# Opening phase of a two-layer trunk: query, gates and half of the keys in seven open PSUM banks, adaLN sums two blocks ahead, gates on 128 partitions

## The chip, the cores and the metric

The kernel runs on one core of one Trainium2 chip. Everything is float32 in HBM. The metric is the device time of one execution in microseconds (us), from a median over several runs. TensorE (PE) multiplies matrices, VectorE (DVE), ScalarE (ACT) and GpSimd (POOL) work on tiles, and SyncE (SP) issues the loads.

## The reference, cut to what matters

A trunk of two layers on 512 tokens of width 1024. Layer 0 mixes the tokens with an mLSTM, layer 1 with a gated MLP; each is followed by a channel MLP. The change touches only the beginning of layer 0:

```python
c_act = silu(c)
mod = c_act @ ada_w[0] + ada_b[0]                # six vectors of 1024
sh1, sc1, g1, sh2, sc2, g2 = split(mod, 6)
h = rmsnorm(x, norm_g[0, 0]) * (1.0 + sc1) + sh1
p = h @ w_in                                     # (512, 3088)
q, k, v, o, ig, fg = split(p, [512, 1024, 2048, 3072, 3080])
ig = 15 * tanh((ig + b_i) / 15); fg = 15 * tanh((fg + b_f) / 15)
logf = log_sigmoid(fg)                           # 8 heads x 512 tokens
bcum = cumsum(logf)                              # inside each chunk of 128 tokens
# running maximum of ig - bcum in a chunk, then the stabilised weights of the mLSTM
```

## The kernel before, in words

Each product of float32 matrices is made of three products of rounded parts (`mm3`, line 248): both operands are split in a high part `hi` and a rest `lo`, and `hi*hi`, `hi*lo`, `lo*hi` are summed in one PSUM bank. ScalarE casts the high part of a weight tile, VectorE or GpSimd subtracts to get the low part (`conv`, line 221). PSUM has eight banks of 128x512: five of `bank()`, two of `bank2()`, one of `bank3()` (lines 76 to 82). Buffers for loaded blocks of 1 MB (`raw`) are five, buffers for adaLN sums (`R`) two, for converted weights (`whi`, `wlo`) four each.

Everything up to line 647 is pinned: each engine's queue follows the program's order exactly (class `Engine`, line 40 on). Behind `pinned[0] = False` a scheduler orders the instructions of each engine.

The input's 1024 columns are handled as eight blocks k of 128. For each block the columns of scale and shift are sums over 1024 rows of `ada_w`. `ada_load` (line 145) loads 1 MB in two DMAs. `ada_init` and `ada_acc` (lines 152 and 157) multiply eight slices by `cact` and add them in two accumulators: two ScalarE operations and six of VectorE on 128x256. `ada_merge` adds the two on GpSimd, `ada_tr` transposes the two halves on TensorE, and `ada_fin` (line 174) reduces each over its row and makes the two columns in four VectorE operations.

The function `mlstm` (line 531) opens with the load of adaLN block 0, the four tiles of x, the gate weights as four loads of narrow columns into zeroed tiles, and the first 128x512 blocks of the query weights. The tiles of x are normalized (sum of squares on ScalarE, power on GpSimd, scaling on VectorE). In the loop over k (line 623) each engine gets: sums of block k+2, columns of block k+1, load of k+3, scale and shift of block k+1 (`feed`, line 604: ScalarE affine, ScalarE cast, low part on GpSimd), query weights of k+1 (`q_hi` on ScalarE, `q_lo` on GpSimd), the 15 matmuls of block k (gates and four query tiles in five banks), and the two transposes of the sums and four of x (`xT`, line 590) for block k+2. The key projection follows the loop: four column tiles of 24 matmuls each, each in a bank of its own (lines 646 and 677).

The gates leave the loop as rows: 8 heads on partitions, 512 tokens along the row. The log sigmoid is a chain of some 16 operations on 8x512, then four transposes and copies turn it, four products with a triangle of ones make the cumulative sum, and the running maximum is seven steps of doubling distance, each a VectorE maximum and a ScalarE copy (lines 696 to 710). The results go to HBM and come back as broadcasts for the decays (`decay`, line 748). The values' projection (`proj_tm`) runs at the same time, the output gates (`o_unit`, line 801) after it.

## Time and profile before

| | us |
|---|---|
| median of 3 runs | 1270.68 |
| range of the runs | 1267.6 to 1271.62 |
| the profiled execution | 1269.99 |
| its span (first to last instruction) | 1268.2 |

| engine | busy us of the span | share |
|---|---|---|
| PE (matmul) | 1210.4 | 95% |
| PEld (weight load) | 986.0 | 78% |
| DVE | 848.0 | 67% |
| ACT | 619.5 | 49% |
| POOL | 129.2 | 10% |

All durations come from one profiled execution; its own time is the basis of sums, and the median lies 0.69 us above it. A matmul's end is modelled, so two matmuls that overlap in the rows are spaced by their starts. The shares are averages over stages with different limits, so a stage is read by itself. Nearly all instructions carry line 50, the helper that issues them, and are told apart by the names of their tiles: `raw` a loaded block, `r` an adaLN sum, `hhi` and `hlo` the two parts of the activations, `whi` and `wlo` those of weights, `pa` the bank of the sums, `pt` the banks of transposes, `ps` the banks of products.

### The profile page before, as it was taken

To read this page: it belongs to the slowest core of one execution; us is meant where nothing else is said; L and a number is where in the kernel's file an instruction comes from. 1 tells how busy PE (TensorE), PEld (TensorE's weight loads), DVE (VectorE), ACT (ScalarE), POOL (GpSimd) and SP (SyncE) were. 2 spreads that over 40 slices of the span, in tenths; PEclk is the share of its full clock that TensorE was granted. 3 is DMA by queue.
4 is the path that set the end of the run, shared out by engine and by line. 5 is a ranking of instruction groups with operands and counts; after the bars stand their busy time and mean duration, and the time that the engine had idled before them with its cause. 6 is when DMAs were issued, how large, how long until landed. Compare 5 with 4: busy or idle time off the path is not lost.

```text
span 1268.2 us, 15234 instructions
## 1 busy us (share of the span) xinstructions
PE 1210.4 (95%) x5705; PEld 986.0 (78%) x5705; DVE 848.0 (67%) x1360; ACT 619.5 (49%) x1107; POOL 129.2 (10%) x158
## 2 busy tenths in 40 slices
PE   2999998999999999999899999999999999999997
PEld 1678777888787887778678788888798888887886
DVE  5897677573967869866666756532747758668545
ACT  4545535285555545553653644322664554545432
POOL 4601211010000000010110023300100000000000
PEclk9999999999999999999999999999999999999999
DMA  9957942433354363365256644332443332331401
GB/s 262 307 185 193 264 127 89 141 125 103 105 166 133 101 198 111 93 213 176 97 154 212 206 119 137 128 108 67 133 133 108 109 125 66 122 111 51 148 1 67
DMA packets 165722, 174.24 MB, mean 137 GB/s; under 512 B 6152, under 2 KB 121080, under 8 KB 165648
## 3 DMA queue, kind: packets, MB, share of 16 engines
q1 hardware_dynamic: 165408, 173.17, 44.0%
q8 instruction: 45, 0.74, 0.2%
q14 instruction: 29, 0.24, 0.1%
q10 hardware_dynamic: 240, 0.09, 0.0%
HBM read 171.11 MB, written 2.14 MB: 137 GB/s over the span
## 4 chain that ended last, share of the span: by engine, by line
PE 70%; DVE 11%; DMA 7%; ACT 5%; issue 2%; POOL 2%; SPq 2%; DVEq 0%; POOLq 0%; ACTq 0%
PE ps L50 49%; PE pt L50 21%; DMA raw<-in_ada_w 5%; DVE wlo L50 3%; DVE a L50 3%; DVE r L50 2%; SPq L50 2%; ACT whi L50 2%; ACT j L50 2%; POOL s L50 1%; ACT t L50 1%; DMA a<-in_b_ws 1%; DVE x L50 1%; DMA raw<-in_a_w_in 1%; DVE s L50 1%
## 5 line engine op out<-in xcount | busy, mean ns | idle before, releaser
L50 DVE TENSOR_TENSOR wlo<-raw,whi 128x1024 fp32r<-128x1024 f32 x232 | 284.8, 1232 | 203.0 <-ACT whi L50 197.5
L50 PE MATMUL ps<-whi,a 128*128 128x512 f32 x1312 | 418.9, 394 | 0.5 <-DVE a L50 0.3
L50 ACT CAST whi<-raw 128x1024 fp32r<-128x1024 f32 x232 | 242.4, 1051 | 309.6 <-PE ps L50 220.4
L50 PEld LDWEIGHTS ps<-whi,a 128*128 128x128 f32 x1312 | 246.4, 188 | 61.8 <-DVE a L50 5.4
L50 PE MATMUL ps<-wlo,a 128*128 128x512 f32 x656 | 256.7, 392 | 0.0
L50 DVE SCALAR_TENSOR_TENSOR r<-raw,cact,r 128x256 f32<-128x256 f32 (+1 forms) x256 | 143.7, 599 | 26.1 <-ACT r L50 13.3
L50 PE MATMUL pt<-hhi,whi 128*128 128x512 f32 x384 | 150.7, 392 | 2.2 <-ACT t L50 1.3
L50 PE MATMUL pt<-hhi,wlo 128*128 128x512 f32 x384 | 149.9, 391 | 1.5 <-DVE wlo L50 1.5
L50 PE MATMUL pt<-hlo,whi 128*128 128x512 f32 x384 | 149.5, 389 | 0.0
L50 PEld LDWEIGHTS ps<-wlo,a 128*128 128x128 f32 x656 | 123.6, 188 | 25.3 <-DVE wlo L50 1.2
L50 PE MATMUL ps<-hlo,whi 128*128 128x512 f32 (+1 forms) x360 | 127.7, 355 | 2.4 <-POOL hlo L50 2.4
L50 PE MATMUL ps<-hhi,whi 128*128 128x512 f32 (+1 forms) x360 | 129.1, 359 | 0.3 <-ACT whi L50 0.3
L50 PE MATMUL ps<-hhi,wlo 128*128 128x512 f32 (+1 forms) x360 | 127.5, 354 | 0.7 <-DVE wlo L50 0.7
L50 DVE TENSOR_TENSOR a<-a,a 128x512 fp32r<-128x512 f32 (+2 forms) x162 | 105.1, 685 | 32.0 <-ACT a L50 31.7
L50 PE MATMUL ps<-wlo,hhi 128*128 128x512 f32 x256 | 102.6, 401 | 6.0 <-DVE wlo L50 5.8
L50 PE MATMUL ps<-whi,hhi 128*128 128x512 f32 x256 | 102.7, 402 | 2.1 <-ACT whi L50 2.1
L50 PE MATMUL ps<-whi,hlo 128*128 128x512 f32 x256 | 101.5, 396 | 0.0
L50 ACT CAST a<-a 128x512 fp32r<-128x512 f32 x108 | 63.2, 616 | 53.9 <-POOL a L50 41.8
L50 POOL TENSOR_TENSOR s<-s,mhalf 128x1 f32<-128x1 f32 (+1 forms) x40 | 32.4, 811 | 548.9 <-DVE s L50 541.6
L50 PEld LDWEIGHTS pt<-hhi,whi 128*128 128x128 f32 x384 | 72.1, 188 | 19.0 <-ACT whi L50 2.5
L50 PEld LDWEIGHTS pt<-hhi,wlo 128*128 128x128 f32 x384 | 72.1, 188 | 18.6 <-DVE wlo L50 3.7
L50 PEld LDWEIGHTS pt<-hlo,whi 128*128 128x128 f32 x384 | 72.1, 188 | 14.7
(128 smaller groups left out, 1376.8 us busy)
## 6 DMA issues: line engine op xcount, KB each, us to landing
raw<-in_ffn_w SPq DMA_DIRECT2D x64, 1024.0 KB, 5.1
raw<-in_ada_w SPq DMA_DIRECT2D x64, 512.0 KB, 5.5
raw<-in_ada_w SPq DMA_DIRECT2D x16, 1024.0 KB, 5.1
raw<-in_b_w_in SPq DMA_DIRECT2D x16, 1024.0 KB
raw<-in_a_w_in SPq DMA_DIRECT2D x10, 1024.0 KB, 10.2
raw<-in_b_w_out SPq DMA_DIRECT2D x8, 1024.0 KB, 5.0
raw<-in_a_w_out SPq DMA_DIRECT2D x4, 1024.0 KB, 5.0
x<-in_x SPq DMA_DIRECT2D x4, 512.0 KB, 6.5
```

The costliest lines, as they stand in the source:

```text
L50: r = f(*a, **k)
```

## The change

x is loaded first. Its tiles are normalized, transposed and copied into two `raw` buffers before the loop. The loads of a block are the adaLN block and 768 columns of weights (512 of the query, 256 of the keys), these in two DMAs. The adaLN sum has one accumulator: one ScalarE operation and seven on VectorE; two matmuls with a column of ones take the place of transposes, merge and reduction; scale and norm weight are joined in one operation. The loop has 21 matmuls for each block in seven banks (four query tiles, two key tiles, gates), all low parts are made on VectorE, and the sums of block k+2 are finished and those of k+3 begun in iteration k. Behind the loop two key blocks are left. The gates are turned first, so that the log sigmoid works on 128 tokens x 32; the running maximum is one scan. The adaLN columns of later sublayers go through `ada_fin` and the new `ada_cols`.

```diff
     def ada_fin(ps, l, vs, vc, ng, k):
         s = small(2)
         dve.tensor_reduce(s, ps[:, 0:2 * P].rearrange("p (a b) -> p a b", a=2), axis=AX.X, op=ALU.add)
-        ab = cp.tile([P, 4], F32, tag="ab", name=nm("ab"), bufs=16)
-        dve.tensor_scalar(ab[:, 2:3], s[:, 1:2], abcol(l, vc, k), 1.0, ALU.add, ALU.add)
+        return ada_cols(s, l, vs, vc, ng, k)
+
+    def ada_cols(s, l, vs, vc, ng, k):
+
+        ab = cp.tile([P, 2], F32, tag="ab", name=nm("ab"), bufs=16)
+        dve.tensor_scalar(ab[:, 1:2], s[:, 1:2], abcol(l, vc, k), ngcol(l, ng, k), ALU.add, ALU.mult)
         dve.tensor_add(ab[:, 0:1], s[:, 0:1], abcol(l, vs, k))
-        dve.tensor_mul(ab[:, 1:2], ab[:, 2:3], ngcol(l, ng, k))
...
+        def load(k):
+
+            raws[k] = ada_load(0, 0, 1, k)
+            raw = A(), A()[:, 0:QK - S]
+            ld.dma_start(raw[0], w[k * P:(k + 1) * P, 0:S])
+            ld.dma_start(raw[1], w[k * P:(k + 1) * P, S:QK])
+            qk[k] = [raw]
+
+        def qk_hi(k):
+            hi = wp.tile([P, QK], F32R, tag="whi", name=nm("whi"))
+            act.copy(hi[:, 0:S], qk[k][0][0])
+            act.copy(hi[:, S:QK], qk[k][0][1])
...
+        def init(k):
+            accs_[k] = R()[:, 0:2 * P]
+            act.activation(accs_[k], flat(k, KC - 1), AF.Copy, scale=cact[:, KC - 1:KC])
+
+        def sums(k, js=range(KC - 1)):
+            a = accs_[k]
+            for j in js:
+                dve.scalar_tensor_tensor(out=a, in0=flat(k, j), scalar=cact[:, j:j + 1], in1=a,
+                                         op0=ALU.mult, op1=ALU.add)
+
+        def total(k):
+
+            ps = bank3()
+            for i in range(2):
+                pe.matmul(ps[:, i:i + 1], lhsT=accs_[k][:, i * P:(i + 1) * P], rhs=one, start=True, stop=True)
+            return ps
...
+        x_stat(0)
+        x_stat(1)
+        x_turn(0)
+        x_stat(2)
+        x_turn(1)
+        x_out(0)
+        x_stat(3)
+        x_turn(2)
+        x_out(1)
         pt = bank2()
         for i in range(2):
             pe.transpose(out=pt[:, i * P:(i + 1) * P], in_=pk[:, i, :], identity=ident)
...
+        x_turn(3)
+        init(0)
+        x_out(2)
+        sums(0)
+        dve.tensor_copy(cols, pt[:, 0:2 * P].rearrange("p (a b) -> p a b", a=2))
+        scales = cols[:, 1, 0:96].rearrange("p (a b) -> p a b", b=KC)[:, 1::3, :]
+        dve.tensor_scalar_add(scales, scales, 1.0)
+        x_out(3)
+        sp0 = total(0)
...
+        qk_hi(0)
+        init(1)
+        qk_lo(0)
+        ab = [ada_cols(sp0, 0, 0, 1, 0, 0)]
+        full = feed_hi(0)
+        sums(1, range(3))
+        feed_lo(0, full)
+        sums(1, range(3, KC - 1))
+        wgc += [conv(wg[i]) for i in range(2)]
+        qk_hi(1)
+        init(2)
+        sums(2, range(2))
         for k in range(KC):
+            main(k, range(2))
+            if k + 1 < KC:
+                sp1 = total(k + 1)
+            main(k, range(2, 7))
+            if k + 3 < KC:
+                load(k + 3)
+            if k + 3 < KC:
+                init(k + 3)
+            if k + 1 < KC:
+                ab.append(ada_cols(sp1, 0, 0, 1, 0, k + 1))
+                qk_lo(k + 1)
+                full = feed_hi(k + 1)
             if k + 2 < KC:
-                ada_acc(raws[k + 2], accs_[k + 2], range(6))
+                sums(k + 2, range(2, 4))
             if k + 1 < KC:
-                ab.append(ada_fin(aps, 0, 0, 1, 0, k + 1))
+                feed_lo(k + 1, full)
+            if k + 2 < KC:
+                qk_hi(k + 2)
+                sums(k + 2, range(4, KC - 1))
             if k + 3 < KC:
...
+                sums(k + 3, range(2))
         pinned[0] = False
...
+        ps = bank2()
+        for n in range(NT):
+            pe.transpose(out=ps[:, n * 40:(n + 1) * 40], in_=gt[0:40, n * P:(n + 1) * P], identity=ident[0:40, 0:40])
+        scr = A()
+        fg, e, z, z2 = (scr[:, i * 32:(i + 1) * 32] for i in range(4))
...
+        kps = accs[4:6]
+        for blk in w_cols(w, QK):
+            kps.append(bank())
+            proj_fm(kps[-1], blk, h, slice(0, S))
...
-            pe.matmul(ps[0:8, n * P:(n + 1) * P], lhsT=lft[n], rhs=triu, start=True, stop=True)
+            pe.matmul(ps[0:8, n * P:(n + 1) * P], lhsT=logf[:, n * 8:(n + 1) * 8], rhs=triu, start=True, stop=True)
...
+        cm = A()[0:8]
+        dve.tensor_tensor_scan(cm, low, u, 0.0, ALU.add, ALU.max)
```

## Rows read from the trace of the kernel before

**Rows 1.** Busy time by stage: stretch, length, each engine's busy us (instructions), clock, DMA.
```profile
0.00:28.00 28.00, 4.39 (x15) 2.78 (x16) 15.65 (x33) 11.61 (x21) 12.76 (x29) 1.00 0.91 256
20.00:28.00 8.00, 1.64 (x7) 1.35 (x8) 7.27 (x13) 3.11 (x6) 3.02 (x4) 1.00 1.18 306
28.00:67.20 39.20, 36.31 (x159) 27.25 (x158) 32.74 (x64) 22.46 (x38) 24.05 (x21) 1.00 0.94 277
88.95:135.00 46.05, 45.83 (x209) 36.85 (x208) 33.87 (x70) 25.19 (x68) 8.24 (x24) 1.00 0.76 215
```

**Rows 2.** Timeline of TensorE, loop and keys: start, duration, engine, operation.
```profile
28.03 0.78 PE L50 MATMUL ps<-hhi,whi 128*128 128x512 f32 x1
...
33.47 0.38 PE L50 MATMUL pa<-ident,r 128*128 128x128 f32 x2
33.69 0.60 PE L50 MATMUL pt<-ident,a 128*128 128x128 f32 x4
...
34.05 0.48 PE L50 MATMUL ps<-hhi,whi 128*128 128x512 f32 x1
...
67.18 0.39 PE L50 MATMUL ps<-hhi,whi 128*128 128x512 f32 x1
...
88.94 0.39 PE L50 MATMUL ps<-whi,hhi 128*128 128x512 f32 x1
```

**Rows 3.** TensorE's waits, 28 to 67 us: us in total, times, longest.
```profile
PE ps L50 <- POOL hlo L50: 2.4, 3, 1.1
```

**Rows 4.** Timeline of VectorE's adaLN sums and GpSimd's subtractions beside them.
```profile
9.89 2.46 DVE L50 SCALAR_TENSOR_TENSOR r<-raw,cact,r 128x256 f32<-128x256 f32 x6 [5.77 <-DMA a<-in_a_hnorm_g]
...
35.03 5.08 DVE L50 SCALAR_TENSOR_TENSOR r<-raw,cact,r 128x256 f32<-128x256 f32 x6
...
36.71 1.29 POOL L50 TENSOR_TENSOR hlo<-t,hhi 128x512 fp32r<-128x512 f32 x1 [0.99 <-ACT hhi L50]
```

**Rows 5.** Timeline of ScalarE's queue in the opening.
```profile
5.28 0.52 ACTq L50 DMA_DIRECT2D a<-in_a_hnorm_g  x1
...
8.92 0.32 ACTq L50 DMA_DIRECT2D a<-in_b_b_in  x1
...
10.16 1.04 ACT L50 ACTIVATE j<-x 128x1024 bf16<-128x1024 f32 x1
```

**Rows 6.** Transfers: two of SP's timeline; two of issue to landing (count, size, us).
```profile
2.34 2.70 SPq L50 DMA_DIRECT2D x<-in_x  x4
23.77 2.29 SPq L50 DMA_DIRECT2D a<-in_a_w_in  x1
raw<-in_ada_w SPq DMA_DIRECT2D x30, 512.0 KB, 6.2
x<-in_x SPq DMA_DIRECT2D x4, 512.0 KB, 6.5
```

**Rows 7.** Groups by shape: count, busy us, mean ns, idle before.
```profile
L50 ACT COPY a<-ps 128x512 f32<-128x512 f32 x4 | 2.0, 585 | 0.0
L50 DVE TENSOR_TENSOR wlo<-raw,whi 128x1024 fp32r<-128x1024 f32 x232 | 284.8, 1232 | 203.0 <-ACT whi L50 197.5
L50 ACT CAST whi<-raw 128x1024 fp32r<-128x1024 f32 x232 | 242.4, 1051 | 309.6 <-PE ps L50 220.4
L50 DVE TENSOR_SCALAR ab<-s,cols 128x1 f32<-128x1 f32 x11 | 2.3, 213 | 0.4
```

**Rows 8.** Timeline: the gates' tanh and the products of the cumulative sum.
```profile
64.42 0.68 ACT L50 ACTIVATE a<-ps,bcol 40x512 f32<-40x512 f32 x1
...
93.05 1.04 PE L50 MATMUL pt<-triu,s 128*8 128x128 f32 x8
```

**Rows 9.** Output-gate stage: TensorE's wait in the timeline; two stretches of busy times.
```profile
139.34 0.50 PE L50 MATMUL ps<-whi,hhi 128*128 128x512 f32 x1 [0.87 <-ACT whi L50]
141.00:143.00 2.00, 2.00 (x7) 1.56 (x6) 2.00 (x2) 2.00 (x5) 0.00 (x0) 0.59 0.64 233
143.00:145.00 2.00, 2.00 (x6) 1.57 (x6) 2.00 (x8) 1.98 (x4) 0.00 (x0) 0.56 0.90 245
```

More of the change, by code (lines that the diff above doesn't have):

```diff
@@ L112, in trunk @@
     pool.memset(mhalf, -0.5)
+    one = cp.tile([P, 1], F32, name="one")
+    pool.memset(one, 1.0)
     ck = cp.tile([8, P], F32, name="ck")
@@ L549, in mlstm, with x_stat, x_turn, x_out @@
         pool.memset(bcol, 0.0)
+        for k in range(3):
+            load(k)
+            if k == 0:
+                ld.dma_start(wgr, w.rearrange("(k p) f -> p k f", p=P)[:, :, 3072:3072 + 2 * NH])
         ld.dma_start(bcol[0:8, :], a_b_if[0, 0:8].rearrange("(p a) -> p a", a=1))
         ld.dma_start(bcol[32:40, :], a_b_if[0, 8:16].rearrange("(p a) -> p a", a=1))
[L553 to L568 removed]
+        xT = [rp.tile([P, 4, S], F32, tag="raw", name=nm("raw")) for _ in range(2)]
+        rs, xps = {}, {}
+        def x_stat(t):
+            v = small(1)
+            pool.tensor_scalar_add(v, meansq(xt[t], D), EPS)
+            rs[t] = small(1)
+            pool.tensor_tensor(out=rs[t], in0=v, in1=mhalf[:, 0:1], op=ALU.pow)
+        def x_turn(t):
+            for s in range(2):
+                xn = A()
+                dve.tensor_scalar_mul(xn, xt[t][:, s * S:(s + 1) * S], rs[t])
+                ps = bank()
+                for j in range(4):
+                    pe.transpose(out=ps[:, j * P:(j + 1) * P], in_=xn[:, j * P:(j + 1) * P], identity=ident)
+                xps[t, s] = ps
+        def x_out(t):
+            for s, f in ((0, act.copy), (1, act.copy if t < 3 else dve.tensor_copy)):
+                f(xT[s][:, :, t * P:(t + 1) * P], xps[t, s].rearrange("p (a b) -> p a b", a=4))
+        x_stat(0)
[7 more added lines that the diff above has]
+        x_out(1)
         pt = bank2()
@@ L587, in mlstm @@
-        accs = [bank() for _ in range(5)]
-        qw = [None] * KC
-        def xT(k):
-            ps = bank2()
-            for t in range(NT):
-                pe.transpose(out=ps[:, t * P:(t + 1) * P],
-                             in_=xn[t][k // 4][:, (k % 4) * P:(k % 4 + 1) * P], identity=ident)
-            return ps
-        def q_hi(k):
-            qw[k] = A(F32R), A(F32R)
-            act.copy(qw[k][0], qr[k])
-        def q_lo(k):
-            pool.tensor_sub(qw[k][1], qr[k], f32(qw[k][0]))
@@ L607, in feed, with feed_lo @@
+        def feed_lo(k, full):
             hh, hl = h(k, slice(0, S))
-            act.copy(hh, full)
-            eng.tensor_sub(hl, full, f32(hh))
-        wgc = [conv(wg[i], lo_eng=pool) for i in range(2)]
-        q_hi(0)
-        q_lo(0)
-        feed(0, xT(0), dve)
-        pool.tensor_scalar_mul(bcol, bcol, 1.0 / CAP)
-        ada_start(1)
-        ada_acc(raws[1], accs_[1], range(6))
-        raws.append(ada_load(0, 0, 1, 2))
-        load_q(2)
-        ada_start(2)
-        aps = ada_tr(accs_[1])
@@ L622, in mlstm, with main @@
-        xps = xT(1)
-        for k in range(KC):
+            dve.tensor_sub(hl, full, f32(hh))
+        accs = [bank() for _ in range(5)] + [bank2() for _ in range(2)]
+        wgc = []
+        def main(k, fs):
+            hh, hl = h(k, slice(0, S))
+            for f in fs:
+                cs = slice(f * P, (f + 1) * P)
+                if f < 6:
+                    wh, wl = qk[k][1][:, cs], qk[k][2][:, cs]
+                else:
+                    wh, wl = (x[:, k % 4] for x in wgc[k // 4])
+                mm3(accs[f], wh, wl, hh, hl, k == 0, k == KC - 1)
@@ new lines, in mlstm @@
+        for i in range(2):
+            for o in range(2):
+                pool.tensor_copy(wg[i][:, :, 32 * o:32 * o + NH], wgr[:, 4 * i:4 * i + 4, NH * o:NH * (o + 1)])
+        pool.tensor_scalar_mul(bcol, bcol, 1.0 / CAP)
+        qk_hi(0)
[8 more added lines that the diff above has]
+        qk_hi(1)
```

115 lines of the change are left out of this document (30 added, 85 removed).

## Prediction

> **What bounds the kernel now.** I read the busy times by stage first. Of the first 135 us TensorE is busy 4.39 of 28.00 before the loop over the eight 128-row blocks of the input, 36.31 of 39.20 in that loop, and nearly all of the time in the value projections from 88.95 on [rows 1]. A busy matmul here is not a matmul at its best pace, so the second view is TensorE's own order of time. The 96 matmuls of the key projection run from 67.18 to 88.94 us, 0.227 us apart. The loop runs from 28.03 to 67.18 us, 39.15 us, for 120 matmuls (27.2 us at that pace) and six pairs of column sums and transposes (0.58 us each, from 33.47 to 34.05: 3.5 us). The first iteration's 15 matmuls take 5.44 us where 3.40 would do, 2.0 us more, at the start of steady work [rows 2]. So 39.15 - 27.2 - 3.5 - 2.0 = 6.4 us of the loop are waits. The profile names GpSimd's low halves of the activations as the largest of them [rows 3]. The third view is VectorE's: six of the adaLN multiply-adds take 2.46 us while GpSimd is still, and 5.08 us while GpSimd subtracts 128x512 tiles [rows 4]; in the loop VectorE is busy 32.74 of 39.20 us [rows 1]. So in this stage the shared work of VectorE and GpSimd ends last, and before it a serial opening; later stages end with TensorE, and there an earlier start is carried through.
>
> **The change part by part.**
>
> *Matmuls.* Before, loop and key projection hold 120 + 96 = 216 products. After, 21 per iteration, 168, and 48 in the two key blocks left: 216 again. Nothing is saved here; only waits, transposes and the start can give time. 168 x 0.227 = 38.1 us, 48 x 0.227 = 10.9 us.
>
> *Transposes of x* leave the loop for the opening, where TensorE is nearly idle [rows 1]. Their price there is in the next point.
>
> *Opening.* x is now loaded first, normalized, transposed and copied to SBUF before the loop. ScalarE could start its squares only at 10.16 us, because its queue held a small load that went out at 8.92 us [rows 5], as the third large transfer, the first tile of x, landed (issued 2.34, 6.5 us to landing [rows 6]). After, the third large transfer is the third tile of x, no later: ScalarE is free at about 8.7 us; ends: 5.8 us (the small load before it went out at 5.28 [rows 5]) and 10.2 us. From there I follow the queues in program order. ScalarE: three squares of 1.04 us [rows 5] and their read-outs, the wait for the first transposes, two copies at 0.59 [rows 7], the fourth square: +7.4 us. Then that tile's power on GpSimd (estimate 1.2), two scalings (0.9) and VectorE is free for the seven sums of block 0 at +9.5. They take 7 x 0.41 = 2.9 [rows 4], two short copies 0.7, the last copy of a turned half 0.7, the low half of the weights 0.95, the two columns 0.4: +15.1. ScalarE's affine and cast of the activations add 1.4, VectorE's low half the rest: +16.8. 8.7 + 16.8 = 25.5 us, against 28.03: 2.5 us won; ends 22.6 and 28.
>
> *adaLN sums by a matmul with a column of ones.* Two transposes and a reduction become two products of fp32 with one moving column, each in two passes (the eight passes for four fp32 products show that [rows 8]). Four weight loads at the 0.11 us at which the column transposes follow each other [rows 2] make 0.45 us; ends 0.3 and 0.75. Seven in the loop: 3.2 us.
>
> *VectorE and GpSimd.* GpSimd leaves the loop. VectorE then has per iteration seven sums (2.9 us), the weights' low half of 768 columns (0.95; 1024 last 1.23 [rows 7]), the activations' (0.6, by 512 columns of the same row) and two short column operations (0.4; the longer one 0.21 [rows 7]): 4.8 us. TensorE has 21 x 0.227 + 0.45 = 5.2 us. The cover is 0.4 us thin, so I leave 1.5 us of waits in the loop; ends 0 and the 6.4 us of today.
>
> *Loads.* One iteration now takes 1.375 MB instead of 1.25 (512 columns of weights became 768), and each load of weights is two DMAs: 256 KB and 128 KB. At the 306 GB/s of the stretch 20 to 28 us [rows 1] this is 4.5 us, under 5.2. The buffers for the adaLN blocks are five, two held by x: load k+3 goes out when the sums of k end, about 6 us into iteration k-2, takes some 6.2 us [rows 6], and ScalarE's start of these sums, queued ahead of the next activations, needs it 2 us into iteration k. Three iterations, 15.6 us, against about 14: covered. If it lands late, that ScalarE instruction holds the activations and TensorE behind them.
>
> A rule speaks against the split: the Trainium skill, DMA: Bandwidth & Descriptors, section Bandwidth, asks for transfers of 1 MiB and more, and its fit (section Anatomy of one DMA) gives about 2.3 us for 128 KB by estimate. By it each iteration's load would last 2.3 us longer; the stream of 256 and 512 KB pieces at 306 GB/s shows no such fixed cost.
>
> *Hand-over to the two key blocks.* Their weights are now converted after the pinned part instead of inside it: 0.5 us, ends 0 and 2.3 (one cast and one subtraction of 128x1024 [rows 7]). The gate path shrinks from operations on 8 partitions x 512 to 128 x 32, and the seven maxima become one scan. TensorE is saturated there today, so I give this nothing by itself. The path starts 11 us closer to the end of the key blocks, which is a rival below.
>
> *Later.* In the output-gate stage TensorE waits 0.87 us for a cast and then has a granted clock of 0.59 and 0.56, near the 1.2 GHz level, for 4 us [rows 9]: 0.9 + 1.7 = 2.6 us. ScalarE's cast stands there behind adaLN loads that follow the gate path's loads in SP's queue. That path ends earlier now, but the order of the queues can stay: I take 1.0 us; ends -2.6 (a second stall of that kind) and 2.6.
>
> *Sum.* End of the keys: 25.5 + 2.0 (slow first matmuls) + 38.1 + 3.2 + 1.5 + 10.9 + 0.5 = 81.7 us, against 88.94: 7.2 us. With 1.0 later: 8.2 us. The profiled execution took 1269.99 us, so 1261.8; the median of the runs lies 0.7 above it: **1262.5 us**.
>
> **The rivals.**
>
> *VectorE is the bound (slower).* If the sums keep the pace of 5.08 / 6 = 0.85 us [rows 4], an iteration is 7 x 0.85 + 1.95 = 7.9 us and the loop 8 x 7.9 + 2.0 = 65.2 against 44.8: +20.4 - 8.2 = 12.2 us slower than before, about 1283. It decides from the point where the loop takes 53.0 us, 6.4 per iteration, 0.63 us per sum. For it: VectorE is full in today's loop. Against: the slow sums stand beside GpSimd's subtractions, which go, and where GpSimd is still the pace is 0.41 [rows 4]. Chance 0.05.
>
> *The load stream is the bound.* A 256 KB load occupies SP's queue for up to 2.29 us [rows 6]. If each further piece costs that much, iteration loads last 6.8 us and the last adaLN block lands some 8 x 2.3 = 18 us later than the stream allows today; 8 us of that have slack. About 10 us come back: 1272, no change. For it: the DMA engines have no idle share in the stretch of that stream. Against: they move 306 GB/s in it, so the long issue is the pressure of a full stream and not a price per piece [rows 1]. Chance 0.12.
>
> *TensorE stands behind the gate path.* Today 28.6 us lie between the tanh and the cumulative-sum products [rows 8]; these stand about 4 us behind the end of the keys. After, the tanh comes at about 70.5 us and the same place is 85.8: 15.3 us of cover. An unshortened path would stop TensorE for 13.3 us: 1276. A path over 15.3 us costs something, one over 23.5 us all of the gain. Against it: the operations become far smaller. Chance 0.05.
>
> *More than forecast.* ScalarE is free at its early end (2.9 us) and the stall of the output gates goes (1.6 us more): 1258. Chance 0.13.
>
> **How the numbers follow.** Forecast 0.65, rivals 0.05, 0.12, 0.05 and 0.13. A measurement of this kernel tells a change of 0.3%, 3.8 us, from none: below 1266.9 is faster, above 1274.5 slower. Of the forecast's 0.65 the unknown terms (opening up to 28, waits up to 6.4, hand-over 2.3) put 0.06 within 0.3%. Faster 0.59 + 0.13 = 0.72; within 0.12 + 0.06 = 0.18; slower 0.05 + 0.05 = 0.10. For the range I take the rival on the low side with some waits gone, 1254, and on the high side the forecast with opening and waits at their far ends, 1270; beyond lie most of the two slower cases and of the load stream, about 0.2.
>
> **What would show it.** The first 128x512 product at 25.5 us; iterations 5.2 to 5.6 us apart; six sums in about 2.5 us all through the loop and no GpSimd work in it; the column sums 0.45 us each; the last key product near 81.7 us, the first value product right behind it. The forecast is wrong if the loop starts after 28 us, if ScalarE waits for adaLN blocks ahead of the activations, or if a stall behind 82 us eats the lead.

## The result and the profile after

| | before | after |
|---|---|---|
| median of the runs, us | 1270.95 | 1256.2 |
| range of the runs | 1267.6 to 1271.62 | 1255.82 to 1256.6 |
| span of the profiled execution | 1268.2 | 1254.2 |

The ratio is 0.9889 with a 95% interval of 0.9871 to 0.9907: 14.1 us faster by the ratio, 14.7 by the medians. The forecast was 1262.5, with a range of 1254 to 1270. (The median of before is that of four runs; the first three alone had 1270.68.)

TensorE's order of time in the kernel after (start, duration, operation, in brackets the wait ahead of it); it answers to [rows 2, 8]:

```profile
23.61 0.79 PE L50 MATMUL ps<-hhi,whi 128*128 128x512 f32 x1 [3.28 <-ACT hhi L50]
...
43.23 0.61 PE L50 MATMUL pa<-one,r 128*128 128x1 f32 x4
...
48.57 0.50 PE L50 MATMUL pa<-one,r 128*128 128x1 f32 x4
...
68.76 0.44 PE L50 MATMUL pt<-ident,a 40*128 40x40 f32 x4 [0.83 <-ACT a L50]
69.23 0.50 PE L50 MATMUL ps<-hhi,whi 128*128 128x512 f32 x1
...
80.38 1.04 PE L50 MATMUL pt<-triu,a 128*8 128x128 f32 x8
81.35 0.50 PE L50 MATMUL ps<-whi,hhi 128*128 128x512 f32 x1
```

The first product comes 4.42 us earlier, two column sums of the loop (four passes each) lie one iteration of some 5.3 us apart, the keys begin at 69.23 and the last of them ends at 80.29; the first value product stands at 81.35, behind the cumulative sums.

Busy time by stage of the kernel after (stretch, length, busy us of PE, PEld, DVE, ACT and POOL with their instructions, clock, DMA share, GB/s): slow start, loop, keys, values, output gates. It answers to [rows 1, 9]:

```profile
20.00:28.00 8.00, 4.72 (x15) 3.57 (x16) 7.60 (x18) 3.71 (x7) 0.24 (x1) 0.59 1.18 305
23.61:67.77 44.16, 44.16 (x196) 35.94 (x196) 40.18 (x90) 22.68 (x39) 0.77 (x2) 0.95 1.00 298
67.77:80.29 12.52, 11.65 (x53) 9.25 (x52) 12.10 (x29) 7.05 (x13) 1.92 (x16) 1.00 0.88 302
81.35:127.54 46.19, 45.82 (x204) 37.18 (x203) 32.00 (x59) 26.40 (x65) 10.06 (x10) 1.00 0.85 235
127.54:134.90 7.36, 7.36 (x48) 6.12 (x47) 7.36 (x15) 3.68 (x6) 1.56 (x1) 1.00 0.91 265
```

TensorE is busy through the whole loop, at a mean granted clock of 0.95 (0.59 in the 8 us around its start), and through the stretch of the output gates at 1.00, where [rows 9] show a wait and then 0.59 and 0.56. The two other parts that the forecast watched, VectorE inside the loop and ScalarE's queue in the opening ([rows 4, 5]):

```profile
44.01 0.27 DVE L50 TENSOR_SCALAR ab<-pa,cols 128x1 f32<-128x1 f32 x1
44.20 0.15 DVE L50 TENSOR_TENSOR ab<-pa,cols 128x1 f32<-128x1 f32 x1
44.27 1.01 DVE L50 TENSOR_TENSOR wlo<-a,whi 128x512 fp32r<-128x512 f32 x2
45.20 1.00 DVE L50 SCALAR_TENSOR_TENSOR r<-raw,cact,r 128x256 f32<-128x256 f32 x2
46.11 0.69 DVE L50 TENSOR_TENSOR hlo<-t,hhi 128x512 fp32r<-128x512 f32 x1
46.72 2.44 DVE L50 SCALAR_TENSOR_TENSOR r<-raw,cact,r 128x256 f32<-128x256 f32 x5
...
4.87 0.52 ACTq L50 DMA_DIRECT2D a<-in_a_hnorm_g  x1
7.50 0.32 ACTq L50 DMA_DIRECT2D a<-in_b_b_in  x1
7.88 1.06 ACT L50 ACTIVATE j<-x 128x1024 bf16<-128x1024 f32 x1 [4.89 <-DMA x<-in_x]
```

The first six lines are one iteration of VectorE: two column operations, the low half of the weights in two pieces, two sums, the low half of the activations and five more sums, without a gap. GpSimd is nearly silent in the loop (0.77 us, two instructions).

Where the 14.7 us arise can be read at four marks: the end of the keys, the end of the value products (the transposes of `r` behind them), the first power of the normalization (the first GpSimd power after the output gates begin), and the end.

| mark | before, us | after, us | lead |
|---|---|---|---|
| first product | 28.03 | 23.61 | 4.42 |
| end of the keys | 88.94 | 80.29 | 8.65 |
| end of the value products | 136.42 | 127.54 | 8.88 |
| first power behind them | 154.34 | 139.64 | 14.70 |
| end of the span | 1268.2 | 1254.2 | 14.0 |

So 8.7 us come from the opening, the loop and the keys, which the forecast put at 7.2, and 5.8 from the start of the output gates, which it put at 1.0. Of the 5.8, TensorE has 4.7: from the end of the value products to the first products of 128x129 behind the first output gates it takes 7.36 us, without a wait, where the kernel before takes 12.06. The other 1.1 lie in the short operations of VectorE and ScalarE that lead from there to the power.

### The profile page after: what moved, and what is told of

It is laid out like the page before. It is cut to its first block, busy times and chain, and to the rows that moved or that the text cites. A ratio compares the mean times of both kernels' runs of the same rounds, so it can differ in the third digit from the quotient of the medians.

```text
span 1254.2 us, 15205 instructions
## 1 busy us (share of the span) xinstructions
PE 1207.9 (96%) x5721; PEld 987.6 (79%) x5721; DVE 837.3 (67%) x1344; ACT 618.7 (49%) x1104; POOL 104.4 (8%) x140
## 4 chain that ended last, share of the span: by engine, by line
PE 77%; DVE 9%; ACT 5%; DMA 4%; issue 2%; POOL 2%; SPq 0%; DVEq 0%; POOLq 0%; ACTq 0%
PE ps L50 54%; PE pt L50 22%; DVE wlo L50 3%; DVE a L50 3%; DMA raw<-in_ada_w 2%; DVE r L50 2%; ACT j L50 2%; ACT whi L50 2%; ACT t L50 1%; POOL s L50 1%; DMA a<-in_b_ws 1%; PE pa L50 1%; DVE x L50 1%; DVE s L50 1%; DMA x<-in_x 0%
## 5 line engine op out<-in xcount | busy, mean ns | idle before, releaser
L50 DVE TENSOR_TENSOR wlo<-raw,whi 128x1024 fp32r<-128x1024 f32 x230 | 281.2, 1226 | 198.8 <-ACT whi L50 193.2
L50 PE MATMUL pt<-hhi,whi 128*128 128x512 f32 x400 | 157.0, 393 | 2.2 <-ACT t L50 1.3
L50 PE MATMUL pt<-hhi,wlo 128*128 128x512 f32 x400 | 156.1, 391 | 1.1 <-DVE wlo L50 1.1
L50 PE MATMUL pt<-hlo,whi 128*128 128x512 f32 x400 | 155.8, 389 | 0.0
L50 PE MATMUL ps<-hhi,whi 128*128 128x512 f32 (+1 forms) x376 | 136.1, 362 | 3.6 <-ACT hhi L50 3.3
L50 PE MATMUL ps<-hhi,wlo 128*128 128x512 f32 (+1 forms) x376 | 134.3, 357 | 0.9 <-DVE wlo L50 0.7
L50 PE MATMUL ps<-hlo,whi 128*128 128x512 f32 (+1 forms) x376 | 134.2, 357 | 0.0
L50 PEld LDWEIGHTS pt<-hhi,whi 128*128 128x128 f32 x400 | 75.1, 188 | 19.6 <-ACT whi L50 2.5
L50 ACT CAST a<-a 128x512 fp32r<-128x512 f32 x100 | 58.3, 616 | 53.5 <-POOL a L50 42.1
L50 PEld LDWEIGHTS ps<-hhi,whi 128*128 128x128 f32 x376 | 71.5, 190 | 13.1 <-ACT hhi L50 3.4
```

The lines of the kernel that those rows point to most:

```text
L50: r = f(*a, **k)
```

## Experiments

Where there is only one time of a kernel, it is weighed by its own stage, since behind 200 us the lead of one profiled execution over another changes by 0.4 to 4.1 us without any edit there. One such place: TensorE waits 1.76 us at 203.59 in the kernel after and at 202.65 in `spload`, and then has a granted clock of 0.50 in the first and of 1.00 in the second. A stretch of 3 us behind it, columns as above, of the kernel after:

```profile
206.00:209.00 3.00, 3.00 (x8) 2.41 (x8) 3.00 (x6) 0.36 (x1) 0.00 (x0) 0.50 0.02 5
```

and of spload:

```profile
206.00:209.00 3.00, 3.00 (x15) 2.46 (x14) 3.00 (x6) 0.00 (x0) 0.00 (x0) 1.00 0.00 0
```

### The two halves of the change, each alone

`oldgates` is the kernel after with the whole gate path of before, `newgates` the kernel before with the whole gate path of after. The edit of `oldgates`, shortened ("..." stands for lines left out, here and below); `newgates` has the same pieces the other way round, against the kernel before:

```diff
-            pe.transpose(out=ps[:, n * 40:(n + 1) * 40], in_=gt[0:40, n * P:(n + 1) * P], identity=ident[0:40, 0:40])
...
-        dve.scalar_tensor_tensor(out=e, in0=fg, scalar=-1.0, in1=fg, op0=ALU.mult, op1=ALU.min)
-        act.activation(e, e, AF.Exp)
+        fg = A()[0:8]
...
+        act.activation(e, fg, AF.Abs)
+        act.activation(e, e, AF.Exp, scale=-1.0)
...
+            pe.transpose(out=ps[:, n * 8:(n + 1) * 8], in_=logf[:, n * P:(n + 1) * P], identity=ident[0:8, 0:8])
...
-        dve.tensor_tensor_scan(cm, low, u, 0.0, ALU.add, ALU.max)
+        for i, s in enumerate((1, 2, 4, 8, 16, 32, 64)):
...
+            dve.tensor_tensor(out=nv[:, :, s:], in0=cv[:, :, s:], in1=cv[:, :, :P - s], op=ALU.max)
+            act.copy(nv[:, :, :s], cv[:, :, :s])
```

> The changed kernel with the gate path of before put back (log sigmoid on 8 partitions x 512, four transposes and copies, seven doubling steps for the maximum); opening, loop and key blocks stay as changed. Theory A: the output-gate stall went because the gate path is short, so its broadcast loads leave SP's queue earlier. Then the results of the gates leave for HBM at 100 us or later instead of 91.8, TensorE waits again in the output gates, and the time is about 4.7 us above the changed kernel, 1260 to 1263 us. Theory B: the stall went with the earlier start alone or with another order that the scheduler chose. Then 1256 to 1257.5 us and no wait there.

Measured: 1268.93 us, ratio to before 0.9996 (0.9985 to 1.0007). Of 14.1 us nothing is left: 12.7 more than the kernel after. Both theories missed the size: the first expected about 4.7, the second next to nothing. What the first said would be seen came (the results leave for HBM at 111.01, TensorE waits again).

> The kernel before with the new gate path alone (gates turned first, log sigmoid on 128 x 32, maximum by one scan); opening, loop and four key blocks as before. Theory A: the wait of TensorE in the output gates at 138 to 147 us goes, the keys still end at 88.9 us: 1265 to 1267 us. Theory B: 1270 to 1271.5 us, the wait stays.

Measured: 1269.66, ratio 1.0003 (0.9993 to 1.0012): no gain. The first theory fell, and of the second only the time came (0.3 under its range): the wait that it expected in the output gates is gone, as is shown below. In the medians each half alone is worth nothing that these runs can tell, and together they are worth 14. At the first power the profiled executions of oldgates and newgates are 1.8 and 1.3 us ahead of before (152.56 and 153.01 against 154.34).

The rows tell why. In `oldgates`, TensorE's two long waits, and ScalarE ahead of the second:

```profile
114.25 0.52 PE L50 MATMUL pt<-ident,a 96*128 96x96 f32 x4 [2.64 <-ACT a L50]
...
139.90 0.80 PE L50 MATMUL ps<-whi,hhi 128*128 128x512 f32 x1 [3.40 <-ACT whi L50]
...
128.38 0.65 ACT L50 COPY a<-ps 128x256 f32<-128x256 f32 x2 [4.79 <-PE ps L50]
128.91 5.09 ACT L50 ACTIVATE a<-a,a 128x128 f32<-128x128 f32 x17
133.91 0.62 ACT L50 COPY a<-ps 128x256 f32<-128x256 f32 x2
134.42 4.49 ACT L50 ACTIVATE a<-a,a 128x128 f32<-128x128 f32 x15
138.81 3.87 ACT L50 CAST whi<-raw 128x1024 fp32r<-128x1024 f32 x4
```

First TensorE stands 2.64 us for the end of the gate path itself (the transposes of its three results). Then it reaches the output gates at 136.5, and their weights are uncast: ScalarE takes its queue in order, and ahead of the casts stand 32 exponentials of the decay tiles. Their input is the gate path's result, which goes through HBM and comes back as broadcasts; GpSimd had masked the first of these by 125.97. ScalarE took them only from 128.91 on, behind a copy that waited 4.79 us for TensorE, and then without a break but for two copies. So the order of the queue has a part in it beside the late path.

In `newgates` the same exponentials stand ahead of another cast, the last one that the second half of the values needs (ScalarE, then TensorE):

```profile
116.57 0.70 ACT L50 ACTIVATE a<-a,a 128x128 f32<-128x128 f32 x2 [2.77 <-POOL a L50]
117.17 0.62 ACT L50 COPY a<-ps 128x384 f32<-128x384 f32 x2
117.69 4.21 ACT L50 ACTIVATE a<-a,a 128x128 f32<-128x128 f32 x14
121.80 1.03 ACT L50 CAST whi<-raw 128x1024 fp32r<-128x1024 f32 x1
...
122.88 1.22 PE L50 MATMUL ps<-whi,hhi 128*128 128x512 f32 x2 [2.74 <-ACT whi L50]
```

From the end of the values to the first power `newgates` takes 12.12 us (140.89 to 153.01) like the kernel after (12.10), where the kernel before takes 17.92. So the stall of the output gates is gone there too, 5.8 us, and with it the first theory was right on the mechanism; but the values end 4.47 us later than before, by the wait of 2.74, six products at half clock behind it (0.2 us each) and a key phase that began 0.40 later.

In the kernel before itself the stall has another cause than in `oldgates`, and it is the one that the prediction read. No exponentials stand ahead of the cast, but an adaLN operation whose load had not landed (ScalarE):

```profile
137.85 0.51 ACT L50 ACTIVATE r<-raw,cact 128x256 f32<-128x256 f32 x1 [4.04 <-DMA raw<-in_ada_w]
138.26 1.03 ACT L50 CAST whi<-raw 128x1024 fp32r<-128x1024 f32 x1
```

SyncE's queue there issues the broadcasts from 110.27 on and four adaLN loads behind them from 124.47 on, for 11.56 us. TensorE's wait of 0.87 follows, then 0.79 and 0.61 for low halves (140.64 and 147.22), and slow products in between.

### Is it ScalarE's queue? The same kernels with the exponentials later

`newlate`, against newgates: the first two decay tiles are emitted later.

```diff
                 prep.step()
+                if cb and t == 0:
+                    decay(0)
+                    decay(1)
...
-            decay(2 * cb)
-            decay(2 * cb + 1)
+        decay(2)
+        decay(3)
```

> The kernel before with the new gate path, as in newgates, and one thing moved: in the second half of the value projection, ScalarE's exponentials of the first two decay tiles are emitted behind the first row block, so that the fourth cast of that half's weights stands in ScalarE's queue ahead of twelve of the fourteen exponentials that it stood behind in newgates. Nothing else changes its place. Theory A (newgates gained nothing because ScalarE, which takes its queue in order, stood 2.77 us for the first broadcast and then did 14 exponentials in 4.21 us before the cast at 121.80, so TensorE stood for 2.74 us at 120.15 and ran slow products behind it): the cast ends before 120, both go, 2.7 + about 2 us: 1264 to 1266. Theory B (the lead is taken by the broadcasts' arrival or by the transfer stream, whatever ScalarE's order): the wait only moves, 1268 to 1271.

Measured: 1267.97 us, ratio 0.9991 (0.9981 to 1.0). In the trace the cast stands at 119.11, and the wait of 2.74 has become 0.68 and 0.76. From the start of the keys to the first power the kernel takes 82.97 us, newgates 85.43, before 87.16: the mechanism is where the first theory put it, with 2.5 us instead of 4.6. The median is 1.7 below newgates, between the two expectations, but the two intervals overlap, so the time by itself shows no gain; the profiled execution also began its keys 1.40 us later than newgates, with 18 products at half clock in its loop against 6.

`oldgates_late`, against oldgates: decay tiles three and four behind the first output-gate unit.

```diff
+            if cb == 0:
+                decay(0)
+                decay(1)
-            decay(2 * cb)
-            decay(2 * cb + 1)
...
                 o_unit(i // 4, i % 4)
+                if i == 0:
+                    decay(2)
+                    decay(3)
```

> The kernel oldgates (the kernel after with the whole gate path of before) with one thing moved: the loads and the 16 exponentials of the third and fourth decay tiles are emitted behind the first unit of the output gates, so that the four casts of the output gates' first weights stand behind 16 exponentials in ScalarE's queue and not behind 32 (two more table loads of 1.28 us come with it, later). Theory A (the 12.7 us that oldgates lost are ScalarE's queue: its exponentials start with the broadcasts at 128.91, and the casts behind them end 3.40 us after TensorE needs them): the wait of 3.40 at 136.5 goes, and the slow products behind it; the 2.64 at 111.6, where TensorE itself stands for the gate path, stays: 1262 to 1265. Theory B (the loss comes from the broadcasts and the weights behind them in SyncE's queue, so a later cast would only be late for another reason): 1267 to 1270.

Measured: 1267.58 us, ratio 0.9985 (0.9974 to 0.9996), inside the second theory's range; it is 1.35 below oldgates, with intervals that overlap. In the trace both had a part of it. The casts begin at 134.28 and the wait of 3.40 is gone, so ScalarE's queue did hold TensorE there; but a new one stands where the second decay tiles are used:

```profile
134.28 1.05 ACT L50 CAST whi<-raw 128x1024 fp32r<-128x1024 f32 x1
...
153.67 2.56 PE L50 MATMUL ps<-a,a 64*128 64x128 f32 x16 [2.66 <-DVE a L50]
```

A late path can be put behind other work at one place and is then late at the next. In these two kernels the order of the queue decided where TensorE waits, and the length of the path that it does.

### Which part of the gate path

`oldls` is the kernel after with the log sigmoid of before alone, `oldmx` with the doubling maxima alone (the part of the edit of oldgates above its scan, or the scan and what replaces it).

> The kernel after with the log sigmoid of before alone (on 8 partitions with 512 elements each, then transposes of it); the scan stays. Theory A (the gate path's length decides): in oldgates VectorE ends the log sigmoid at 94.5 us, in the kernel after at 78.1, 2.3 us ahead of the end of the keys, so about 14 us of path come back on the far side of the keys; the maxima are still the scan. Most of the 12.7 us that oldgates lost: 1262 to 1266. Theory B (what oldgates lost is the order of the queues that it happened to get, not the length): any value from 1256 to 1270, and not between those of oldmx and oldgates.

> The kernel after with the seven doubling maxima of before in place of the scan; the log sigmoid stays new. Theory A (length): from the cumulative sums' copy to the last of the gate operations VectorE takes 16.6 us in oldgates and 10.8 in the kernel after, so the path ends 5.8 us later, at about 98 us; the output gates' second weights are issued at 128 instead of 122, just as TensorE needs them (it reaches the output gates at 127.9): 1256 to 1260. Theory B (order of queues): not tied to the length; a stall of 2 to 3 us with slow products behind it, 1260 to 1264, would speak for it.

Measured: oldls 1257.13, ratio 0.9904 (0.9889 to 0.9918); oldmx 1255.52, ratio 0.9887 (0.9872 to 0.9902). Neither can be told from the kernel after. For oldls the first theory's 1262 to 1266 fell: the path became longer by 11 us, not 14, and that much was nearly free. For oldmx the time is 0.5 under the first theory's range, the path is 4.8 us later instead of 5.8, and the stall of the second theory did not come. Set out by when the gate path is written to HBM (first write, from the queue of loads):

| kernel | written at, us | broadcasts from | keys' start to first power | median |
|---|---|---|---|---|
| after | 89.91 | 94.11 | 70.4 | 1256.2 |
| oldmx | 94.68 | 98.10 | 71.0 | 1255.52 |
| oldls | 100.81 | 104.94 | 73.6 | 1257.13 |
| oldgates | 111.01 | 114.82 | 82.5 | 1268.93 |

The first 11 us of lateness cost 3.2 us at the first power, of which the median keeps 0.9, less than its runs can tell; the next 10 cost 8.9 there and 11.8 in the median. In oldls ScalarE's first cast for the output gates starts at 127.79, just behind the last exponential, and TensorE passes there with one wait of 0.78: its margin is used up, and nearly all that comes on top is paid. That is why the parts cost next to nothing singly and 12.7 together. One thing stays open: singly the parts make the path 10.9 and 4.8 us later, together 21.1; where the other 5.4 come from no run here shows.

The log sigmoid is the larger part. On 8 partitions with 512 elements a reciprocal takes 3.33 us, and the chain ends at 94.46 in oldgates; on 128 partitions with 32 elements it ends at 78.19, 2.1 us before the keys do. VectorE in oldgates:

```profile
75.95 3.33 DVE L50 RECIPROCAL a<-a 8x512 f32<-8x512 f32 x1
...
93.79 0.67 DVE L50 SCALAR_TENSOR_TENSOR a<-a,a 8x512 f32<-8x512 f32 x1
```

and in the kernel after, with the scan behind it:

```profile
77.55 0.64 DVE L50 SCALAR_TENSOR_TENSOR a<-a 128x32 f32<-128x32 f32 x3
...
84.46 1.21 DVE L50 TENSOR_TENSOR_SCAN a<-a,a 8x512 f32<-8x512 f32 x1
```

### VectorE in the loop

`gplo` gives both low halves of blocks 1 to 7, weights and activations, to GpSimd:

```diff
+            eng = pool if k else dve
...
-            dve.tensor_sub(lo[:, 0:S], raw[0], f32(hi[:, 0:S]))
+            eng.tensor_sub(lo[:, 0:S], raw[0], f32(hi[:, 0:S]))
... (the same for the other 256 columns)
-            dve.tensor_sub(hl, full, f32(hh))
+            (pool if k else dve).tensor_sub(hl, full, f32(hh))
```

> The changed kernel with the low parts of weights and activations of blocks 1 to 7 made on GpSimd, as before the change. Theory: GpSimd's subtractions of 128x512 slow VectorE's multiply-adds (0.49 us each now) to 0.6 to 0.85 us and take twice VectorE's time themselves, so an iteration goes from 5.27 us to 5.8 to 6.5: 1260 to 1266 us. Rival: the loop gained by transposes and serial adaLN steps that left it, and VectorE has room: at most 1257.5 us and iterations of 5.3 us.

Measured: 1262.49, ratio 0.9951 (0.9933 to 0.9969): 6.3 us slower than the kernel after, as expected of contention. VectorE is left with less work and needs longer for it (timeline of VectorE, then of GpSimd):

```profile
41.78 5.78 DVE L50 SCALAR_TENSOR_TENSOR r<-raw,cact,r 128x256 f32<-128x256 f32 x7
...
43.44 1.52 POOL L50 TENSOR_TENSOR hlo<-t,hhi 128x512 fp32r<-128x512 f32 x1 [2.12 <-ACT hhi L50]
44.93 2.35 POOL L50 TENSOR_TENSOR wlo<-a,whi 128x512 fp32r<-128x512 f32 x2
```

and TensorE's waits of 28 to 68 us (total, times, longest), the answer to [rows 3]:

```profile
PE ps L50 <- POOL hlo L50: 1.6, 4, 0.4
```

Seven sums take 5.78 us, 0.83 each, as in [rows 4]; in the kernel after, without GpSimd beside them, they take 0.49. From 34 to 64 us VectorE is busy 28.92 of 30 us and GpSimd 20.39, so it is VectorE that sets the pace. Iterations are 5.95 us apart instead of 5.27, and the keys begin 5.5 us later.

`extra1` adds one multiply-add per iteration, into a tile that nobody reads.

```diff
+            for _ in range(1):
+                dve.scalar_tensor_tensor(out=waste, in0=xt[0][:, 0:2 * P], scalar=cact[:, 0:1], in1=waste, ...)
```

> The kernel after with one more multiply-add of 128x256 on VectorE in each of the eight iterations, into a tile that nobody reads. It measures the cover. Theory A (TensorE is the bound of the loop with VectorE 35.40 of 39.20 us busy, 0.47 us free per iteration): 0.41 to 0.49 us more per iteration is still hidden, iterations stay at 5.27 us, the last product of the loop moves by 0 to 1.5 us. Theory B (VectorE's lead is already used up, as a chain through ScalarE's activations): each iteration grows by 0.3 to 0.5 us, the end of the loop by 2.5 to 4 us.

Two column sums of TensorE, one iteration apart, then the added operation and the sums behind it in VectorE's queue:

```profile
50.40 0.61 PE L50 MATMUL pa<-one,r 128*128 128x1 f32 x4
55.85 0.60 PE L50 MATMUL pa<-one,r 128*128 128x1 f32 x4
...
46.91 0.48 DVE L50 SCALAR_TENSOR_TENSOR a<-x,cact,a 128x256 f32<-128x256 f32 x1
47.30 1.00 DVE L50 SCALAR_TENSOR_TENSOR r<-raw,cact,r 128x256 f32<-128x256 f32 x2
```

Measured in the trace: iterations 5.45 us apart instead of 5.27. By the starts of VectorE's rows the added operation takes 0.40 us of its queue and costs 0.18, so the cover (what VectorE can take on in an iteration before TensorE waits) was 0.22 us: between the two theories, and thinner than the 0.4 of the forecast. (The keys begin 2.3 us later, about 1.4 of it by more products at half clock at the start; the one time, 1254.33, says nothing about the loop.)

`twoacc` lets two accumulators take turns and adds them at the end.

```diff
-            accs_[k] = R()[:, 0:2 * P]
-            act.activation(accs_[k], flat(k, KC - 1), AF.Copy, scale=cact[:, KC - 1:KC])
+            accs_[k] = R()
+            for j in (KC - 2, KC - 1):
+                act.activation(accs_[k][:, (j % 2) * 2 * P:(j % 2 + 1) * 2 * P], flat(k, j), AF.Copy, scale=cact[:, j:j + 1])
... (the multiply-adds take the halves in turn, one addition joins them)
```

> The changed kernel with two accumulators for each adaLN sum, taken in turn, and one addition of the two at the end (six multiply-adds and one addition instead of seven, one more ScalarE operation). Theory: a multiply-add that reads what the one just before wrote waits for it, 0.49 us apart instead of 0.41; then the spacing in this kernel is 0.41 again, the seven operations of block 0 take about 2.8 us instead of 3.6, and the loop, bound by TensorE, keeps 5.27 us: 0.5 to 1 us faster. Rival: the spacing of 0.49 comes from other traffic and stays, no gain.

Measured once: 1254.17 us, span 1252.4. Six sums take 2.46 us in its opening, 0.41 each, where the kernel after needs 3.60 for seven, 0.51 each; the first product comes 0.75 us earlier. But iterations stay at 5.27, as long as TensorE needs for one, and 1.76 us are lost again at 113.59 to a late cast of the kind seen in newgates. What lies behind 200 us makes up the rest of its time, so this run shows the pace and nothing on the whole.

### The opening

`adafirst` loads the first adaLN block ahead of x.

```diff
+        raw0 = ada_load(0, 0, 1, 0)
         for t in range(NT):
             xx = xp.tile([P, D], F32, tag="x", name=f"x{t}")
...
-            raws[k] = ada_load(0, 0, 1, k)
+            raws[k] = ada_load(0, 0, 1, k) if k else raw0
```

> The kernel after with the first adaLN block (512 KB) loaded ahead of x instead of behind it, as the kernel before does. It measures what of the earlier first product (23.61 us against 28.03) comes from x being first. Theory A (the opening is a chain that begins with x on ScalarE): the first square starts 1.3 to 1.7 us later and the first product comes at 24.9 to 25.3. Theory B (the chain begins with the sums, that is, with the adaLN block): first product at 23.6 or earlier.

Measured in the trace: first square at 9.30 instead of 7.88, first product at 25.05 instead of 23.61. The first theory holds: the chain of the opening begins with x on ScalarE, and 1.44 of the 4.42 us come from the order of these loads. In both kernels the first square follows at once on the issue of a small load from ScalarE's queue (at 7.50 in the kernel after, at 8.93 here), so the order of the large loads acts through that issue. The one time is 1254.5; the lead that it lacks at 198 us (1.86) is made up behind.

`better2` was meant to beat the kernel after. It moves the two small loads and reorders VectorE's work; two accumulators and the read-outs of the last turned tile, both on ScalarE, come with it. Its edit in words, not line by line:

```diff
-    act.dma_start(pk[64:72, 0, :], a_hnorm_g...); act.dma_start(pk[72:88, 0, :], b_b_in...)
+        x_stat(1); act.dma_start(pk[64:72, 0, :], a_hnorm_g...); act.dma_start(pk[72:88, 0, :], b_b_in...)
-    sums(0) ahead of cols; init(1) and qk_lo(0) ahead of block 0's columns; first sums(1) ahead of feed_lo(0)
+    cols ahead of sums(0); block 0's columns ahead of qk_lo(0); feed_lo(0) ahead of init(1) and sums(1)
```

> The kernel after with its opening put in another order, and two accumulators for the adaLN sums: the two small loads on ScalarE's queue go behind its first two squares, the turned columns of the parameters are read before the first sums instead of behind them, both read-outs of the last turned tile are ScalarE's, and block 0's columns and activations come ahead of block 1's sums on VectorE. Theory A (each us of the opening is carried to the end, as in the kernel after): ScalarE's squares start 0.5 to 1.5 us sooner, the two waits of VectorE's chain shrink, first product at 21.5 to 22.9 instead of 23.61, and the time 0.7 to 2.5 us below the 1256.2 of the kernel after: 1253.7 to 1255.5. Theory B (a later stage sets the end again, as the waits at 648 and 656 us let one guess): 1256 to 1257, though the first product is earlier.

Measured: 1259.22, ratio 0.9923 (0.9911 to 0.9936): 3.0 us slower than the kernel after. Both theories fell. The first square does come at 4.99, but then the moved loads hold the third one (ScalarE):

```profile
11.05 0.52 ACTq L50 DMA_DIRECT2D a<-in_a_hnorm_g  x1
12.83 0.32 ACTq L50 DMA_DIRECT2D a<-in_b_b_in  x1
13.25 1.06 ACT L50 ACTIVATE j<-x 128x1024 bf16<-128x1024 f32 x1 [5.75 <-DMA raw<-in_ada_w]
```

The second square ended at 7.5; the next issue went out only at 11.05. The profile puts the wait of 5.75 us down to the landing of an adaLN block; why the issue was held no run here shows. The first product stands at 24.52, 0.91 later than in the kernel after, the start of the loop has 15 products at half clock against 8, and the keys begin some 2.9 us later; a late cast costs TensorE another 1.78 us at 116.00. Of the parts of this edit only the moved loads were then tried alone.

`spload` therefore takes both loads off ScalarE's queue and changes nothing else:

```diff
-    act.dma_start(pk[64:72, 0, :], a_hnorm_g...); act.dma_start(pk[72:88, 0, :], b_b_in...)
...
             ld.dma_start(xx, x[0, t * P:(t + 1) * P, :])
             xt.append(xx)
+        ld.dma_start(pk[64:72, 0, :], a_hnorm_g...); ld.dma_start(pk[72:88, 0, :], b_b_in...)
```

> The kernel after with one thing moved: the two small loads of parameters that stood on ScalarE's queue ahead of the first square (the second went out at 7.50 us) go to SyncE's queue, behind the four loads of x. Every engine's order of work stays. Theory A (ScalarE is held by those two issues, as better2 showed, where the first square came at 4.99 and the two loads, moved behind the second square, held the third until 13.25; and the opening is a chain from the squares on): first square at 5.0 to 6.0 us, first product 1.5 to 2.9 us earlier, at 20.7 to 22.1, and 0.7 to 2.9 us of time: 1253.3 to 1255.5. Theory B (the two issues only change the queue in which they are held, and SyncE's loads of the first adaLN block and weights come so much later that the chain begins there): first product at 23 to 24.5, 1255.5 to 1258.

Measured: 1252.5, ratio 0.9856 (0.9837 to 0.9876), 3.7 us below the kernel after and the fastest here (0.8 under the first theory's range); the two intervals just overlap. ScalarE and TensorE:

```profile
5.17 1.06 ACT L50 ACTIVATE j<-x 128x1024 bf16<-128x1024 f32 x1 [2.23 <-DMA x<-in_x]
...
20.98 0.79 PE L50 MATMUL ps<-hhi,whi 128*128 128x512 f32 x1 [3.28 <-ACT hhi L50]
...
27.57 0.51 ACT L50 ACTIVATE r<-raw,cact 128x256 f32<-128x256 f32 x1 [4.19 <-DMA raw<-in_ada_w]
...
29.49 0.49 PE L50 MATMUL ps<-hhi,whi 128*128 128x512 f32 x1 [1.20 <-ACT hhi L50]
```

The first theory's mechanism is shown: the first product is 2.63 us earlier. On SyncE's queue the two small loads go out at 3.09 and 3.63. The load that stays on ScalarE's queue ahead of the first square (`ada_b`) goes out later, at 4.76 instead of 3.45, so ScalarE is still held for a part of the time. But the keys begin only 0.57 earlier. For one iteration the load stream is now late: ScalarE waits 4.19 us for an adaLN block, ahead of the next activations in its queue, and TensorE waits 1.20 behind it. Of the profiled gain of 2.3 us, 1.0 stands at the first power, and 1.4 more arise at the clock at 206 us shown above. How much of the 3.7 us the moved loads own is left open.

## Why the prediction was right, and where it was not

*End of the keys.* Forecast 81.7, measured 80.29, term by term:

| term | forecast | measured |
|---|---|---|
| first product | 25.5 | 23.61 |
| slow first matmuls | 2.0 | 2.5 |
| 168 products | 38.1 | 38.1 |
| column sums | 3.2 | 3.5 |
| waits in the loop | 1.5 | 0 |
| hand-over | 0.5 | 1.5 |
| 48 key products | 10.9 | 11.1 |

One reading carried the loop: that VectorE and GpSimd were in each other's way there, and that this is most of the 6.4 us of TensorE's waits (gplo, which sets them side by side again, brings the keys back by 5.5 us). The transposes that left the loop gave TensorE nothing: six pairs at 0.58 were 3.5 us before, and the seven column sums, at 5.27 - 21 x 0.227 = 0.50 each, are 3.5 after. What they did to the engines beside TensorE was not tried alone. With the opening (4.42) and the waits (6.4), less the slow first matmuls (0.5), the hand-over (1.5) and the slower key products (0.2), the lead at the end of the keys is 8.6 of the 8.65 measured.

*Opening.* The direction and the reason, ScalarE's start behind a small load, were right (adafirst, spload); the size was off by 1.9 us, still inside its bounds. ScalarE was free at 7.88 instead of 8.7, and the chain from the first square on took 15.7 us instead of 16.8.

*VectorE.* The sums were put at 0.41 us; they take 0.49, on one accumulator. Work per iteration is 5.1 (44.01 to 49.11) and not 4.8, the cover 0.22 (extra1) and not 0.4. It held all the same, so the 1.5 us of waits did not come. The slower rival did not occur; its pace is that of gplo, 0.83 us per sum beside GpSimd.

*Loads.* 1.375 MB per iteration (1.44 million bytes: 4.7 us at 306 GB/s, where the forecast had 4.5) went through in iterations of 5.26 to 5.34 us. ScalarE waited once for an adaLN block ahead of the activations, 2.37 us at 39.14, which the prediction had named as a sign of being wrong; TensorE did not stand for it, and the iterations kept their length. The rival of the load stream did not occur: the loop moved 298 GB/s in pieces of 128 to 512 KB, and no iteration became 2.3 us longer. The Trainium skill, DMA: Bandwidth & Descriptors, section Bandwidth, asks for transfers of 1 MiB and more. The Trainium skill's fit in section Anatomy of one DMA of the same page, from which the prediction's estimate of 2.3 us came, is for loads that GpSimd issues, and these go out from SyncE. The trace does not show the price of that estimate, and no run loads the same bytes in larger pieces, so the rule itself is not tried here. That the stream is near its bound shows in spload.

*Hand-over.* The forecast gave 0.5 us and the keys began 1.5 behind the loop: TensorE waits 0.83 for ScalarE's tanh, because the transposes of the gates stand ahead of the keys in its queue, and the transposes themselves take 0.44. The sum had counted neither.

*Later.* This is the term that was mis-sized: "the order of the queues can stay: I take 1.0 us; ends -2.6 and 2.6". Measured are 5.8 us, outside both ends. The mechanism was read rightly, a cast behind adaLN loads that follow the gate path's loads, and it went when the path ended earlier (newgates and the kernel after). But the row read for it [rows 9] was the first of three waits (0.87, 0.79 and 0.61) and its slow products; the stage from the end of the values to the first power, 17.92 us before and 12.10 after, was not read as a whole. And "I give this nothing by itself" of the gate path was right only by itself (newgates: nothing).

*The gate path as a rival.* An unshortened path that stops TensorE for 13.3 us comes near the measured 12.7 of oldgates, but by another mechanism, so the nearness is luck: TensorE does not stop at the cumulative sums, which the scheduler placed among the value products; it stops at the path's end and at casts behind the path's exponentials. Its point of decision did not hold either. In oldls 26.8 us lie between the tanh (68.24) and the cumulative-sum products (95.05); by the prediction a path over 23.5 us costs all of the gain, yet the median is only 0.9 us higher (the first power comes 3.4 us later).

So the forecast, 8.2 us, was low by 6.5: 1.4 of it in opening, loop and keys and 4.8 at the output gates; the remaining 0.3 are what is won and lost behind, and the medians against the profiled executions. The time lies inside the stated range, but nearer to the rival "More than forecast" (1258, chance 0.13: ScalarE early and the stall of the output gates gone) than to the case with the chance of 0.65; of that rival's conditions the second came by more than its size, and of the first's 2.9 us 0.8.

## What to carry to other kernels

Find the second chain beside the busy engine (here gates, HBM, broadcasts, exponentials, casts) and measure its margin at the place where the two meet: here shortening either alone gave nothing that the runs can tell, and the gain appeared when both were shortened. A queue that is taken in order makes the casts of the next stage wait for whatever late work stands ahead of them; read what the wait of that queue is put down to, for the same stall was a late load in the kernel before and exponentials of a late path in oldgates. And issue small loads from the queue of an engine that computes nothing (spload: first product 2.63 us earlier; how much of it reaches the end is open).

## What the runs showed of the hardware

- Multiply-adds of VectorE that follow each other on the same accumulator are 0.49 us apart, on two in turn 0.41 (128x256; the kernel after and twoacc). Beside GpSimd's subtractions of 128x512 they are 0.83 apart (gplo).
- The running maximum by a scan takes 1.21 us for 8x512 (the kernel after), where most others of that shape (TENSOR_TENSOR, SCALAR_TENSOR_TENSOR) take 0.67 (oldgates). The Trainium skill, DVE: opcode table, instruction layouts, handler registers and perf-mode slots, section Datapath and trigger behaviour, says that this scan runs at half throughput; the trace agrees (1.21 against 0.67).
- An issue of a load of a few KB stood 3.5 us on ScalarE's queue (better2, 7.5 to 11.05) while large transfers were running.
- Behind a wait of 1.76 us TensorE had a granted clock of 0.50 for 3 us in one profiled execution (the kernel after) and 1.00 in another (spload), with the same work ahead of it.
